# A planner that holds lone attention steps until a second one is ready, and transposes two heads at once

## The chip, the cores and the metric

One Trainium2 chip, one of its cores. The time is the device time of one execution in microseconds (us); a kernel's time is the median of its runs. The kernel before takes 402.29 us (three runs, 402.02 to 402.58). The core has five engines that matter here: TensorE (PE, matrix products and transposes), VectorE (DVE), ScalarE (ACT), GpSimd (POOL) and SyncE (SP, which only issues the DMAs here).

## The reference

The function is a decoder trunk of two layers on 256 tokens of width 1024, in fp32, and a last RMSNorm. Each layer has a mixer and a cross-attention on a memory of 256 rows:

```python
def rms_norm(x, g):
    y = x * lax.rsqrt(jnp.mean(x * x, axis=-1, keepdims=True) + RMS_EPS)
    return y * g
# mixer: one projection of rms_norm(x) to 4096 columns, three attentions beside each other
#   MoBA, 6 heads of 64: at 256 tokens plain causal softmax(q k^T / 8) v
#   differential, 4 heads: (softmax1 - lam * softmax2) v, then a per-head rms_norm
#   stick-breaking, 6 heads: A[t,s] = sigmoid(z_ts) * prod_{s<j<t} (1 - sigmoid(z_tj)), then A v
# each result times silu(its gate columns), all joined; x = x + joined @ w_out
# cross: q = rms_norm(x) @ w_xq, k and v = rms_norm(mem) @ w_xkv, 4 heads of 128, softmax; x = x + ... @ w_xo
```

## The kernel before

**Products.** Each fp32 operand is split in a high and a low part in the reduced type fp32r (`whi`, `wlo` for weights, `xh`, `xl` for activations); each product is made as three, high·high, high·low, low·high. Weights arrive in granules of 128x1024 (`wraw`), each of which ACT turns into `whi` (L155) and DVE into `wlo` (L156). `w_stationary` (L389) makes a group of 512 output columns in 96 products of 256 columns each; `t_stationary` (L416 to L418), `mixed` and the memory projections (L485 to L487 for V) use products of 512 columns.

**What is woven into them.** Attention, norms and score work is written as generators ("jobs"), which the planner in `job`, `tick` and `finish` steps. The planner has a clock `now` in ns of its own. After every 12 products of `w_stationary` the code calls `tick(1310)`, after 6 of `t_stationary` the same, after 3 of the V projection `tick(650)`. A tick adds that to the clock and steps each job whose due time has come, until `JOB_SHARE` ns of work are issued. A step issues its instructions into PE's order at that place, and yields how long it counts for and how long to wait until the next: `PT_WAIT` after the transposes of probabilities, `COMBINE_NEXT` and `MOBA_NEXT` between the first head's and the second head's. `finish(*js)` steps the named jobs to their end with no regard to due times.

The order that comes out is PE's own program order and is fixed before the run. DVE's and ACT's orders are made by a scheduler from its own estimates and from the marks `urgent()`.

**The norm.** A row norm needs the sum of squares over channels. `rstd` does it in two steps. Step A: two transposes of `sqacc` on PE (L350), a reduction on DVE (`ssx`, L353), then `inv_root`: `msx` on DVE (L333), Ln and Exp on ACT (L334, L335), `rtx` in three small operations on DVE (L339 to L341), `rsx` (L342). Step B: two transposes of `rsx` on PE (L358) and a copy to SBUF (`rbcx`, L361), by which projections are multiplied. `rstd` waits `RSTD_WAIT` = 4300 or, in the cross part, `X_RSTD` = 1600 between A and B. In the mixer `finish(njob)` stands behind the gate groups W2 and W3 (192 products, the rest of that norm is forced there), in the cross part behind `memory_v(l, 0)`.

**The mixer.** Order of projections: W2, W3 (gates), W0, M (stick-breaking q, k, v), T0 (differential q, k), T3, T2, T1, the memory's K, then the output O0, O1 in three parts, of which each is preceded by a `finish` of the attention whose results it takes: `finish(*jobs)` for the stick-breaking (`jobs`), `finish(*dj)` for the differential (`dj`), `finish(*mj)` for MoBA (`mj`).

- `sb(c)`: three pairs of heads; scores (`stick_banks`), `softplus` with its splits `sbh`, `sbl` (L168, L169), then `stick_weights` (L620, L621), Exp to `pt`, then values (`pv`, L568 and L570 in all three attentions).
- `diff(c)`: scores (L533), numerators, the combination on DVE, then `p_transposed` for each of two heads (three transposes L557 and the copy to `pt` on ACT, L560), values, the squares' transposes `sums`, and `diff_norm`.
- `moba(c)`: three pairs of heads; scores, numerators, two `p_transposed`, values.

**The cross part.** XQ (96 products), half of V, the forced norm, for each head `xq = bank * rbcx` (L876) and its split, the other half of V woven with score steps (L893 to L902), transposes, `ptl`, then the values (L923), and the output XO or, in the last layer, `last_products` (L988).

In the code and the profile a product number counts projection products of PE from the start, one for each matmul of a projection.

Of the kernel before, what the change touches and what calls it, by code (L numbers as in the profile page):

```python
# [54 lines left out]
ORDER = [(l, g, i) for l in range(DEPTH) for g, i in LAYER]  # L55
N_GRAN = {"O0": 4, "O1": 4, "XQ": 4, "K": 4, "V": 4, "XO0": 2, "XO1": 2}
N_GRAN.update({g: 4 for g in IN_GROUPS})
JOB_SHARE = 1200
SB_WAIT, SB_PACE = 8000, 9000
DIFF_WAIT, DIFF_PACE, COMBINE_WAIT, COMBINE_NEXT = 6500, 8500, 3750, 1700  # L60
MOBA_WAIT, MOBA_PACE, MOBA_NEXT = 5200, 2000, 1100
X_WAIT, PT_WAIT, ROPE_WAIT = 6000, 950, 8800
NORM_WAIT, FIRST_NORM, DN_AFTER = 12500, 10000, 6000
GAINS = dict(attn=0, xattn=16, mem=32)
LOOKAHEAD = 5
# [1 line left out]
Q_WAIT, Q_PACE, XPT_WAIT = 950, 450, 3100  # L67
MEM_WAIT, MEM_NORM, X_RSTD = 6000, 28000, 1600
MOBA_START, SB_START, DIFF_START = 14350, 1500, 1000
PT_LAST = 1300  # L70
MIX_NORM = 14000
HALVED = 5
SQ_WAIT = 5100
# [3 lines left out]
class Trunk:  # L77
# [36 lines left out]
    def tick(self, ns):  # L114

        self.now += ns
        done = 0.0
        for j in list(self.jobs):
            if j[0] <= self.now and done < JOB_SHARE:
                t = self.now  # L120
                self._step(j)
                done += self.now - t
# [505 lines left out]
    def mixer(self, l):  # L628
# [67 lines left out]
        def together(pending, last, first, then):  # L696

            pending.append((first, then))
            if last:
                outs = [f() for f, _ in pending]  # L700
                for o, (_, f) in zip(outs, pending):
                    f(o)
# [34 lines left out]
        def diff(c):  # L737

            self.finish(tj)
            qk = []  # L740
            for s in range(4 * c, 4 * c + 4):
                cb, r = s // 4, 32 * (s % 4)
                qk.append([x[r:r + 32, cb * 256:cb * 256 + 256] for x in dT])
            pr = [self.numerators(ps, 32 ** -0.5) for ps in self.score_quad(qk)]
            yield 1100, DIFF_WAIT
            for j in range(2):
                (p1, r1), (p2, r2) = pr[2 * j:2 * j + 2]
                nc.vector.tensor_scalar(r2, r2, self.lam[:, l:l + 1], None, OP.mult)
                for t, cc in ((0, slice(0, 128)), (1, slice(128, 384))):
                    nc.vector.tensor_scalar(p2[:, cc], p2[:, cc], r2[:, t:t + 1], None, OP.mult)  # L750
                    nc.vector.scalar_tensor_tensor(p1[:, cc], p1[:, cc], r1[:, t:t + 1], p2[:, cc],
                                                   OP.mult, OP.subtract)
            yield 0, COMBINE_WAIT
            pts = []
            for j in range(2):
                pts.append(self.p_transposed(pr[2 * j][0]))
                yield 330, (PT_WAIT if j else COMBINE_NEXT)
            sq = []

            def gated(o):  # L760
                q2 = self.work.tile([128, 256], F32, name="sq")
                nc.scalar.activation(q2, o, AF.Square)
                g = self.gate[3 + len(sq)]
                nc.vector.scalar_tensor_tensor(g, o, self.hg[:, l:l + 1], g, OP.mult, OP.mult)
                sq.append(q2)

            dp.append((pts, c))
            if c == 0:
                return
            outs = [self.pv(lambda j, t: tok["t2"][:, t, 256 + 64 * (2 * c + j):320 + 64 * (2 * c + j)], pts)  # L770
                    for pts, c in dp]
            for o in outs:
                gated(o)
            yield 1440, 2600
            sums = self.bank()
            for i, q2 in enumerate(sq):
                for t in range(2):
                    nc.tensor.transpose(sums[:, i * 256 + t * 128:i * 256 + t * 128 + 128],
                                        q2[:, t * 128:t * 128 + 128], self.ident)
            nc.vector.tensor_reduce(pm, sums.rearrange("p (i d) -> p i d", d=64), AX.X, OP.add)  # L780
            yield 440, 0
# [15 lines left out]
        tok["t3"] = token("T3", "t3")  # L797

        dj = [self.job(diff(c), DIFF_START + DIFF_PACE * c) for c in range(2)]
        t2 = tok["t2"] = token("T2", "t2")  # L800
        self.rope(t2[:, :, 0:256], 4, 64, 8, 0)
# [8 lines left out]
        def moba(c):  # L810
            self.finish(tj2, tj3)
            if c != 1:

                for i in ((0, 1), (), (2,))[c]:
                    qk = [x[64 * j:64 * j + 64] for j in range(2) for x in (blk(i), blk(3 + i))]
                    mq[i] = self.score_banks(*qk)
            ps = []
            for b in mq[c]:
                p, r = self.numerators(b, 0.125)
                for t, cc in ((0, slice(0, 128)), (1, slice(128, 384))):  # L820
                    nc.vector.tensor_scalar(p[:, cc], p[:, cc], r[:, t:t + 1], None, OP.mult)
                ps.append(p)
            yield (1520, 0, 760)[c], MOBA_WAIT
            pts = []
            for j in range(2):
                pts.append(self.p_transposed(ps[j]))
                yield 330, (PT_LAST if j else MOBA_NEXT)
            together(mp, c > 0, lambda: self.pv(lambda j, t: tok["t3"][:, t, 64 * (2 * c + j):64 * (2 * c + j) + 64],
                                                pts),
                     lambda o: nc.vector.tensor_tensor(self.gate[c], o, self.gate[c], OP.mult))  # L830
            yield 640 * len(mp) * (c > 0), 0
            if c:
                mp.clear()

        mj = [self.job(moba(c), MOBA_START + MOBA_PACE * c) for c in range(3)]
        dj.append(self.job(diff_norm(), DN_AFTER))
        self.memory_k(l)
# [274 lines left out]
```

## Time and profile before

| what | value |
|---|---|
| median of 3 runs | 402.29 us (402.02 to 402.58) |
| the profiled execution | 402.34 us, span of its records 400.6 us |
| mean granted clock of TensorE | 0.999 of full speed |
| PE busy | 392.7 us, 98% of the span |
| DVE, ACT busy | 316.1 us (79%), 277.8 us (69%) |
| HBM | 62.55 MB read, 159 GB/s over the span |

The span is 1.74 us shorter than the time of that execution; what lies around it doesn't change with the order of the work. An instruction's start in a timeline is followed by its duration; those of matmuls overlap, so what one costs PE is the distance between two starts. Where a row has `xN`, N instructions of that form follow each other and the duration is of all. In brackets stands how long the engine was idle before the instruction, and who ended that.

### The profile page before, as it was taken

The numbers are of one execution on the slowest core, as the hardware profiler recorded it, in microseconds if no ns is written. First come the engines' busy times: TensorE is split into PE (matmuls) and PEld (weight loads), VectorE is DVE, ScalarE is ACT, GpSimd is POOL, SyncE is SP. The second block draws the span as 40 slices with busy tenths as digits, with TensorE's granted clock in tenths as the row PEclk, the third lists the DMA queues.
The fourth block names the chain that finished last, engine by engine and source line by source line (L and its number), as shares of the span: only waits on it lengthen the run. The fifth ranks groups of instructions, "written<-read, shape, count | busy, mean of one in ns | idle before, by whom it ended". The sixth has DMA issues, their size and how long they took to land.

```text
span 400.6 us, 7730 instructions
## 1 busy us (share of the span) xinstructions
PE 392.7 (98%) x2819; PEld 356.9 (89%) x2819; DVE 316.1 (79%) x786; ACT 277.8 (69%) x587; POOL 41.1 (10%) x105
## 2 busy tenths in 40 slices
PE   8999999999999999999999999999999999999993
PEld 8999988877899989988999999888788999998983
DVE  5978959788967869879796864786997796797964
ACT  7979678776855768549485934879686567674843
POOL 4687930000000000000000000000000000000000
PEclk9999999999999999999999999999999999999999
DMA  8995784433354343721737674443256423361002
GB/s 273 360 321 164 248 318 132 146 107 130 136 179 137 106 148 116 235 82 52 261 116 262 232 234 160 157 159 107 90 160 219 155 91 130 107 205 59 1 2 105
DMA packets 19190, 64.10 MB, mean 160 GB/s; under 512 B 2384, under 2 KB 2768, under 8 KB 19152
## 3 DMA queue, kind: packets, MB, share of 16 engines
q1 hardware_dynamic: 19152, 63.61, 47.2%
q8 instruction: 22, 0.36, 0.4%
q14 instruction: 16, 0.13, 0.1%
HBM read 62.55 MB, written 1.05 MB: 159 GB/s over the span
## 4 chain that ended last, share of the span: by engine, by line
PE 92%; DVE 3%; DMA 2%; ACT 1%; issue 1%; SPq 0%; DVEq 0%; ACTq 0%
PE bank L389 41%; PE bank L416 8%; PE bank L418 7%; PE bank L417 7%; PE bank L988 3%; PE bank L568 2%; PE bank L557 2%; PE bank L923 1%; PE bank L486 1%; PE bank L485 1%; PE bank L487 1%; PE bank L620 1%; DMA wraw<-in_memT_dram 1%; PE bank L726 1%; PE bank L444 1%; PE bank L443 1%
## 5 line engine op out<-in xcount | busy, mean ns | idle before, releaser
L156 DVE TENSOR_TENSOR wlo<-wraw,whi 128x1024 fp32r<-128x1024 f32 (+2 forms) x118 | 137.2, 1169 | 38.7 <-ACT whi L155 38.0
L155 ACT ACTIVATE whi<-wraw 128x1024 fp32r<-128x1024 f32 (+2 forms) x118 | 118.5, 1011 | 41.3 <-PE bank L389 21.0
L389 PE MATMUL bank<-xh,whi 128*128 128x256 f32 x416 | 119.5, 289 | 0.2 <-ACT xh L306 0.2
L389 PE MATMUL bank<-xh,wlo 128*128 128x256 f32 x416 | 117.5, 284 | 0.0
L389 PE MATMUL bank<-xl,whi 128*128 128x256 f32 x416 | 117.1, 283 | 0.0
L389 PEld LDWEIGHTS bank<-xh,whi 128*128 128x128 f32 x416 | 79.8, 193 | 1.7 <-issue 0.7
L389 PEld LDWEIGHTS bank<-xh,wlo 128*128 128x128 f32 x416 | 79.9, 193 | 0.0
L389 PEld LDWEIGHTS bank<-xl,whi 128*128 128x128 f32 x416 | 79.6, 192 | 0.0
L416 PE MATMUL bank<-whi,xh 128*128 128x512 f32 x128 | 52.1, 407 | 0.0
L417 PE MATMUL bank<-wlo,xh 128*128 128x512 f32 x128 | 50.1, 391 | 0.0
L418 PE MATMUL bank<-whi,xl 128*128 128x512 f32 x128 | 50.0, 391 | 0.0
L547 ACT ACTIVATE prob<-prob,mx 128x128 f32<-128x128 f32 (+1 forms) x56 | 24.8, 445 | 10.9 <-DVE mx L544 10.9
L416 PEld LDWEIGHTS bank<-whi,xh 128*128 128x128 f32 x128 | 24.0, 188 | 6.2 <-issue 2.0
L418 PEld LDWEIGHTS bank<-whi,xl 128*128 128x128 f32 x128 | 24.0, 188 | 5.4
L417 PEld LDWEIGHTS bank<-wlo,xh 128*128 128x128 f32 x128 | 24.1, 188 | 4.1
L306 ACT ACTIVATE xh<-h 128x256 fp32r<-128x256 f32 x32 | 14.5, 497 | 6.6 <-DVE h L302 6.3
L389 PE MATMUL bank<-mh,whi 128*128 128x256 f32 x64 | 18.9, 296 | 0.0
L542 DVE CUSTOM_DVE_ANT_0 prob<-bank,cmask 128x128 f32<-128x128 f32 (+1 forms) x56 | 17.9, 351 | 0.3
L389 PE MATMUL bank<-ml,whi 128*128 128x256 f32 x64 | 18.1, 283 | 0.0
L389 PE MATMUL bank<-mh,wlo 128*128 128x256 f32 x64 | 18.1, 282 | 0.0
L317 ACT ACTIVATE sq<-h 128x256 f32<-128x256 f32 x28 | 11.4, 411 | 6.6 <-DVE sqacc L318 6.2
L608 DVE SCALAR_TENSOR_TENSOR sbr<-sbe,sbr 128x384 f32<-128x384 f32 x12 | 6.4, 555 | 11.8 <-ACT sbr L607 11.8
(268 smaller groups left out, 780.0 us busy)
## 6 DMA issues: line engine op xcount, KB each, us to landing
wraw<-in_w_dram SPq DMA_DIRECT2D x107, 512.0 KB, 3.6
wraw<-in_w_dram SPq DMA_DIRECT2D x10, 256.0 KB, 4.6
wraw<-in_memT_dram SPq DMA_DIRECT2D x4, 512.0 KB, 4.8
h<-in_xT_dram SPq DMA_DIRECT2D x3, 256.0 KB, 4.9
out_dram<-wraw SPq DMA_DIRECT2D x2, 288.0 KB, 2.2
wraw<-in_gfin_dram SPq DMA_DIRECT2D x1, 512.0 KB, 4.7
out_dram<-wraw SPq DMA_DIRECT2D x2, 224.0 KB, 2.2
h<-in_xT_dram SPq DMA_DIRECT2D x1, 280.0 KB, 3.2
```

The costliest lines, as they stand in the source:

```text
L155: nc.scalar.activation(hi[:, c], raw[:, c], AF.Copy)
L156: nc.vector.tensor_tensor(lo[:, c], raw[:, c], hi[:, c].bitcast(F32), OP.subtract)
L306: nc.scalar.activation(h, src[k], AF.Copy, scale=g)
L317: nc.scalar.activation(s, src[k], AF.Square)
L389: nc.tensor.matmul(outs[m], st[:, kk, c], x[k], start=k + p == 0 and m % 2 == 0, stop=k == n - 1 and p == 2, skip_group_check=True)
L416: nc.tensor.matmul(outs[t], xh[k][:, c], whi[:, kk, :], start=first, stop=False)
L417: nc.tensor.matmul(outs[t], xh[k][:, c], wlo[:, kk, :], start=False, stop=False)
L418: nc.tensor.matmul(outs[t], xl[k][:, c], whi[:, kk, :], start=False, stop=last)
L542: nc.vector.tensor_tensor_reduce(s[:, c], ps[:, c], self.cmask[:, c], 1.0, -3.0e38, OP.add, OP.max, accum_out=m[:, t:t + 1])
L547: nc.scalar.activation(s[:, c], s[:, c], AF.Exp, bias=m[:, t:t + 1], scale=scale, accum_out=sm[:, t:t + 1])
L557: nc.tensor.transpose(ps[:, b * 128:b * 128 + 128], p[:, b * 128:b * 128 + 128], self.ident)
L988: nc.tensor.matmul(out[:, 0:w], x[:, r], w_, start=m == 0 and not seeded, stop=m == 11, skip_group_check=True)
```

## The change

`tick` looks first at how many jobs are due. If it is exactly one, and it came due less than `HOLD` = 2700 ns ago by the planner's clock, the tick does nothing. Otherwise it steps as before. `finish` is not touched. In `diff` and `moba` the transposes of both heads are issued in one step, at the time at which the second head's was issued before or, by the hold, later. `PT_WAIT` goes from 950 to 1400, `PT_LAST` from 1300 to 1500.

```diff
-JOB_SHARE = 1200
+JOB_SHARE, HOLD = 1200, 2700
...
-X_WAIT, PT_WAIT, ROPE_WAIT = 6000, 950, 8800
+X_WAIT, PT_WAIT, ROPE_WAIT = 6000, 1400, 8800
...
-PT_LAST = 1300
+PT_LAST = 1500
...
         self.now += ns
+        ready = [j[0] for j in self.jobs if j[0] <= self.now]
+        if len(ready) == 1 and self.now - ready[0] < HOLD:
+            return
         done = 0.0
...
             yield 0, COMBINE_WAIT
-            pts = []
-            for j in range(2):
-                pts.append(self.p_transposed(pr[2 * j][0]))
-                yield 330, (PT_WAIT if j else COMBINE_NEXT)
+            yield 0, COMBINE_NEXT
+            pts = [self.p_transposed(pr[2 * j][0]) for j in range(2)]
+            yield 660, PT_WAIT
...
             yield (1520, 0, 760)[c], MOBA_WAIT
-            pts = []
-            for j in range(2):
-                pts.append(self.p_transposed(ps[j]))
-                yield 330, (PT_LAST if j else MOBA_NEXT)
+            yield 0, MOBA_NEXT
+            pts = [self.p_transposed(p) for p in ps]
+            yield 660, PT_LAST
```

Every engine has the same instructions as before; only their order differs. On PE the stretches of other work between projection products become 52, from 67. The line numbers of the kernel after are 3 higher (L350 is L353 there, L358 is L361, L389 is L392).

First place: the norm of the mixer in layer 0, where group W3 ends and W0 begins. PE before (`xh_303`, `xl_304` are the last channel block of W3, `xh_275` the first of W0); step A stands 48 products earlier:

```order
L389 MATMUL bank<-xh_303,whi 128x256
L389 MATMUL bank<-xh_303,wlo 128x256
L389 MATMUL bank<-xl_304,whi 128x256
L358 MATMUL bank<-ident,rsx 128x128 x2
L389 MATMUL bank<-xh_275,whi 128x256
L389 MATMUL bank<-xh_275,wlo 128x256
L389 MATMUL bank<-xl_276,whi 128x256
```

PE after, the same place:

```order
L392 MATMUL bank<-xh_303,whi 128x256
L392 MATMUL bank<-xh_303,wlo 128x256
L392 MATMUL bank<-xl_304,whi 128x256
L353 MATMUL bank<-ident,sqacc 128x128 x2
L361 MATMUL bank<-ident,rsx 128x128 x2
L392 MATMUL bank<-xh_275,whi 128x256
L392 MATMUL bank<-xh_275,wlo 128x256
```

Step A has moved to the forced `finish`, directly in front of step B. DVE before, from the reduction of step A on:

```order
L353 TENSOR_REDUCE ssx<-bank 128x2
L156 TENSOR_TENSOR wlo<-wraw,whi 128x1024
L333 TENSOR_SCALAR msx<-ssx 128x2
L156 TENSOR_TENSOR wlo<-wraw,whi 128x1024
L339 TENSOR_TENSOR rtx<-rsx 128x2
L340 TENSOR_TENSOR rtx<-rtx,msx 128x2
L341 TENSOR_SCALAR rtx<-rtx 128x2
L156 TENSOR_TENSOR wlo<-wraw,whi 128x1024
L342 TENSOR_TENSOR rsx<-rsx,rtx 128x2
L156 TENSOR_TENSOR wlo<-wraw,whi 128x1024
L361 COPY rbcx<-bank 128x256
```

DVE after (`ml` is the low part of the memory's activations, which before stood behind `rbcx`); `ssx` and one `wlo` stand ahead of these rows:

```order
L336 TENSOR_SCALAR msx<-ssx 128x2
L310 SCALAR_TENSOR_TENSOR ml_634<-wraw,h,mh_633 128x256
L310 SCALAR_TENSOR_TENSOR ml_638<-wraw,h,mh_637 128x256
L310 SCALAR_TENSOR_TENSOR ml_642<-wraw,h,mh_641 128x256
L342 TENSOR_TENSOR rtx<-rsx 128x2
L310 SCALAR_TENSOR_TENSOR ml_646<-wraw,h,mh_645 128x256
L343 TENSOR_TENSOR rtx<-rtx,msx 128x2
L310 SCALAR_TENSOR_TENSOR ml_650<-wraw,h,mh_649 128x256
L344 TENSOR_SCALAR rtx<-rtx 128x2
L310 SCALAR_TENSOR_TENSOR ml_654<-wraw,h,mh_653 128x256
L345 TENSOR_TENSOR rsx<-rsx,rtx 128x2
L310 SCALAR_TENSOR_TENSOR ml_658<-wraw,h,mh_657 128x256
```

Six operations of the memory's split now stand between `msx` and `rsx`. Second place: ACT in layer 0 while the third pair of stick-breaking heads is made ready (`sbh` is its split, `t_1303` the token group T3). Before:

```order
L607 ACTIVATE sbr<-sby 128x384
L728 ACTIVATE dT_1149<-bank 128x512
L155 ACTIVATE whi<-wraw 128x1024
L168 ACTIVATE sbh<-sbe 128x384
L686 ACTIVATE t_1303<-bank,rsx 128x512 x2
L168 ACTIVATE sbh<-sbe 128x384
L728 ACTIVATE dT_1150<-bank 128x512
L155 ACTIVATE whi<-wraw 128x1024
L624 ACTIVATE pt<-bank 128x384 x2
```

And after:

```order
L731 ACTIVATE dT_1102<-bank 128x512
L608 ACTIVATE sby<-sbe 128x384
L689 ACTIVATE t_1303<-bank,rsx 128x512
L171 ACTIVATE sbh<-sbe 128x384
L610 ACTIVATE sbr<-sby 128x384
L689 ACTIVATE t_1303<-bank,rsx 128x512
L158 ACTIVATE whi<-wraw 128x1024
L627 ACTIVATE pt<-bank 128x384
L171 ACTIVATE sbh<-sbe 128x384
L627 ACTIVATE pt<-bank 128x384
```

The second head's `sbr` and `sbh` have moved behind the two halves of `t_1303` and a `whi`. Third place: PE in the cross part of layer 0, in the first half of the V projection. Before:

```order
L487 MATMUL bank<-whi,ml_646 128x512
L350 MATMUL bank<-ident,sqacc 128x128 x2
L485 MATMUL bank<-whi,mh_649 128x512
L486 MATMUL bank<-wlo,mh_649 128x512
L487 MATMUL bank<-whi,ml_650 128x512
L485 MATMUL bank<-whi,mh_653 128x512
L486 MATMUL bank<-wlo,mh_653 128x512
L487 MATMUL bank<-whi,ml_654 128x512
L485 MATMUL bank<-whi,mh_657 128x512
L486 MATMUL bank<-wlo,mh_657 128x512
L487 MATMUL bank<-whi,ml_658 128x512
```

And after:

```order
L490 MATMUL bank<-whi,ml_658 128x512
L488 MATMUL bank<-whi,mh_661 128x512
L489 MATMUL bank<-wlo,mh_661 128x512
L490 MATMUL bank<-whi,ml_662 128x512
L353 MATMUL bank<-ident,sqacc 128x128 x2
L361 MATMUL bank<-ident,rsx 128x128 x2
L488 MATMUL bank<-whi,mh_633 128x512
L489 MATMUL bank<-wlo,mh_633 128x512
```

Step A has moved 12 products later, to the end of the first half of V, and step B follows it at once; before, nine products stood between them (step B follows the last row of the first of these two). In layer 1 the cross part moves alike.

## Rows read from the trace of the kernel before

**Rows 1.** Page: busy time by engine; share of the chain that ended last

```profile
PE 392.7 (98%) x2819; PEld 356.9 (89%) x2819; DVE 316.1 (79%) x786; ACT 277.8 (69%) x587; POOL 41.1 (10%) x105
...
PE 92%; DVE 3%; DMA 2%; ACT 1%; issue 1%; SPq 0%; DVEq 0%; ACTq 0%
```

**Rows 2.** Windows behind the last product: window, us, busy by engine, PEclk, DMA, GB/s

```profile
394.50:399.50 5.00, 0.00 (x0) 0.00 (x0) 1.53 (x6) 1.65 (x5) 0.00 (x0) 1.00 0.34 130
399.50:400.60 1.10, 0.00 (x0) 0.00 (x0) 0.00 (x0) 0.00 (x0) 0.00 (x0) 0.50 0.00 0
```

**Rows 3.** Chain in order of time, 136 to 150: start us, us, what

```profile
138.24 0.66 PE bank L557 x6
...
143.84 1.63 PE bank L389 x12
145.47 0.33 PE bank L557 x3
145.80 1.43 PE bank L389 x12
```

**Rows 4.** Timeline of PE, first norm: start us, us, instruction

```profile
23.23 0.38 PE L350 MATMUL bank<-ident,sqacc 128*128 128x128 f32 x2
23.37 0.36 PE L389 MATMUL bank<-xh,whi 128*128 128x256 f32 x1
...
29.20 0.38 PE L358 MATMUL bank<-ident,rsx 128*128 128x128 f32 x2
```

**Rows 5.** Timeline of DVE, first norm

```profile
23.65 0.42 DVE L353 TENSOR_REDUCE ssx<-bank 128x2 f32<-128x256 f32 x1 [1.68 <-PE bank L350]
24.00 1.26 DVE L156 TENSOR_TENSOR wlo<-wraw,whi 128x1024 fp32r<-128x1024 f32 x1
25.18 0.16 DVE L333 TENSOR_SCALAR msx<-ssx 128x2 f32<-128x2 f32 x1
...
30.42 3.24 DVE L307 SCALAR_TENSOR_TENSOR ml<-wraw,h,mh 128x256 fp32r<-128x256 f32 x8
```

**Rows 6.** Timeline of ACT, first norm

```profile
29.32 3.31 ACT L306 ACTIVATE mh<-wraw,h 128x256 fp32r<-128x256 f32 x8
```

**Rows 7.** Timeline of PE, norm of the cross part, layer 0

```profile
170.96 0.38 PE L350 MATMUL bank<-ident,sqacc 128*128 128x128 f32 x2
...
173.33 0.43 PE L358 MATMUL bank<-ident,rsx 128*128 128x128 f32 x2
```

**Rows 8.** Timeline of DVE, cross part, layer 0

```profile
173.11 0.16 DVE L342 TENSOR_TENSOR rsx<-rsx,rtx 128x2 f32<-128x2 f32 x1
...
175.00 0.48 DVE L494 SCALAR_TENSOR_TENSOR xvl<-bank,rsm,xv 128x256 fp32r<-128x256 f32 x1
...
181.58 1.21 DVE L156 TENSOR_TENSOR wlo<-wraw,whi 128x1024 fp32r<-128x1024 f32 x1
```

**Rows 9.** Timeline of PE, third stick-breaking pair, layer 0

```profile
84.88 0.34 PE L620 MATMUL bank<-sbh,trim 128*128 128x384 f32 x1
```

**Rows 10.** Timeline of DVE, third stick-breaking pair, layer 0

```profile
81.60 1.21 DVE L156 TENSOR_TENSOR wlo<-wraw,whi 128x1024 fp32r<-128x1024 f32 x1
...
84.39 0.56 DVE L169 TENSOR_TENSOR sbl<-sbe,sbh 128x384 fp32r<-128x384 f32 x1
```

**Rows 11.** Timeline of ACT, third stick-breaking pair, layer 0

```profile
82.56 1.38 ACT L686 ACTIVATE t<-bank,rsx 128x512 f32<-128x512 f32 x2 [0.79 <-PE bank L418]
```

**Rows 12.** Page, costliest groups: count | busy us, mean ns | idle before, releaser

```profile
L155 ACT ACTIVATE whi<-wraw 128x1024 fp32r<-128x1024 f32 (+2 forms) x118 | 118.5, 1011 | 41.3 <-PE bank L389 21.0
```

**Rows 13.** Instructions of line 560: duration min/median/max in ns, first and last start

```profile
L560 ACT ACTIVATE pt<-bank x20: 469/477/491, 103.1 to 340.2; 128x384 f32<-128x384 f32 x20
```

**Rows 14.** Chain, its longest pieces, cross parts of layers 0 and 1

```profile
174.25 0.76 DVE xq L876 x2
...
383.44 11.07 PE bank L988 x60
```

**Rows 15.** Timeline of ACT, norm of the mixer, layer 1

```profile
218.81 0.91 ACT L306 ACTIVATE mh<-wraw,h 128x256 fp32r<-128x256 f32 x2 [1.19 <-DMA wraw<-in_memT_dram]
```

## The prediction

> **What bounds the kernel now.** I read the page's busy times first, then its chain, then timelines of PE, DVE and ACT at each place where PE's order changes. PE is busy for 392.7 of 400.6 us and has 92% of the chain that ended last [rows 1]: nearly everything waits for PE, and PE waits for hardly anything. So the change can gain only by making PE's own work shorter, and it loses wherever a held step makes PE wait, because the products behind a waiting instruction can't pass it. At most 400.6 − 392.7 = 7.9 us of idle PE can go, of which some 6 us are the tail after the last product [rows 2], which the change doesn't touch.
>
> The chain also gives the price of a stop. Six transposes cost 0.66 us and three 0.33, 0.11 each with no fixed part [rows 3]: joining two stops of three saves nothing on PE. Twelve products take 1.43 us, and 1.63 where they follow a values step in fp32 [rows 3]: such a stop has 0.20 us that joining could save.
>
> **The change part by part.** The order of the kernel after gives the places; the prices are from the rows.
>
> A, norm of the mixer, layer 0. Before, step A is at 23.23 and step B at 29.20 [rows 4], with 48 products between, which cost 29.20 − 23.37 = 5.8 us (the two transposes cost PE 23.37 − 23.23 = 0.14 by the next start; their row's 0.38 overlaps). PE never waits there. After, B follows A at once, and PE stands for the whole chain. From A's start: the reduction begins 0.42 later (23.65 − 23.23) [rows 4, 5], takes 0.35 until the next begins; `wlo` takes 1.18 (25.18 − 24.00) [rows 5]; `msx` is thus at +1.95. Behind it DVE's new order has three `ml`, 3.24 / 8 = 0.405 each [rows 5], which end at about +3.3; ACT's Ln and Exp lie beside them, behind `mh` of 3.31 / 8 = 0.41 [rows 6]. Then `rtx`, `ml`, `rtx`, `ml`, `rtx`, `ml`, `rsx`: three `ml` and some 0.15 for each small one bring `rsx` to +4.95. From `rsx` to B it is 0.22 (173.33 − 173.11) [rows 7, 8]: B starts at +5.17. Of this A's own 0.14 was paid before: **+5.0** on PE, with nothing that hides it. If the `ml` come late and the scheduler's order leaves only `wlo` in the way, it is 4.0; with three `mh` ahead of Ln and one `wlo` of waiting, 5.6.
>
> B, third pair of stick-breaking heads, layer 0 (the T3 group's end). Before, the second head's `sbl` began at 84.39 and took 0.56; PE began the block at 84.88 [rows 9, 10], just as it became ready: no slack. After, the block is behind the end of T3 and six products; its weights need the second head's `sbr` and `sbh`, which ACT now has behind the two halves of `t` (1.38) [rows 11], a `whi` of 1.01 [rows 12], and DVE behind a `wlo` of 1.21 [rows 10]. Counted from T3's last product, PE comes to the second head's part at 3.5 and its high part is ready at 5.65, its low part at 6.15: I take **+2.5**. The lower end is 0 (DVE's chain `sbr`, `sbe` isn't delayed if ACT reorders nothing that matters), the upper 3.5, with one more `wlo`. In layer 1 the same pair comes 12 products later and is covered: 0.
>
> C, the differential heads. Both heads' transposes now come together, and values, squares and `diff_norm` 36 products later, in front of the second part of the output, with 48 products left (5.7 us by 1.43 for 12 [rows 3]). The norm of 8 columns, two multiplications and two splits fit under that: 0. If that cover were gone, 0 to 1 in each layer.
>
> D, the last MoBA pair, both layers. Before, twelve products stood between the last head's transposes and its values [rows 3]. After, the forced `finish` puts six transposes directly in front of the values; PE waits for both `pt` copies on ACT, 0.477 us each [rows 13], one behind the other, of which the first begins while PE transposes the second head: 0.33 to fill and 0.477 to leave, **+0.8** each, **1.6** together. With a `whi` ahead of them on ACT it would be 3; with the copies early, 0.6. Queued behind are the last parts of O0 and O1, which need these values.
>
> E, norm of the cross part, both layers. Before, nine products covered most of A to B (170.96 to 173.33) [rows 7], and what followed was a chain on DVE, not on PE: `xq` is a piece of the chain that ended last [rows 14]. After, A comes 12 products later and B at once behind it. A chain bound by latency moves by what its head moves: 12 products of V (nine of them take 2.2 between these rows, some 0.1 of it a restart behind the transposes; twelve take 12 / 9 × 2.1 = 2.8 us), and what PE stands between A and B (173.33 − 170.96 − 0.14 = 2.2) lies inside this. Added to it: an `xvl` of 0.48 and, on its path, part of a `wlo` of 1.21 [rows 8], which the new order has ahead of the splits of `xq` and of `ptl`: 0.6 and 0.6. **+4.0** in layer 0; in layer 1, where last_products follow (11.07) [rows 14] and one `wlo` less is in the way, **+3.6**. Together 7.6; from 5 (only the 2.2 each, and 0.3 of order) to 9.
>
> F, norm of the mixer, layer 1. Here `mh` waited for a DMA of the memory until 218.81 [rows 15], and B waited for it. After, A is 24 products later and B 12 later, so 36 instead of 48 stand between: 4.5 us by program; seven `ml`, two `wlo` (1.2 each) and a `whi` put `rsx` at about +6.1: a stall of 1.6, of which 0.3 was there before: **+1.3**, from 0 (the DMA had set it all) to 2.5.
>
> G, the joined stops. Of fifteen stops less, two have the exit of 0.20 [rows 3]: **−0.4**, from 0 to −1.
>
> Sum: 5.0 + 2.5 + 0 + 1.6 + 4.0 + 3.6 + 1.3 − 0.4 = **+17.6**. On the profiled execution of 402.34 this is **419.9**; the median of the runs, 402.29, is 0.05 below, which doesn't matter here. With all lower ends 4.0 + 0 + 0 + 0.6 + 5 + 0 − 1 = +8.6, **411**; with all upper ends 5.6 + 3.5 + 2 + 3 + 9 + 2.5 + 0 = +25.6, **428**.
>
> **The rivals.**
> The clock falls. PE's granted clock went from 1.00 to 0.50, its lower level of 1.2 GHz, after 5.0 us without a product [rows 2]; the whole run before has no other such fall. In A the gap is 5.17 − 0.38 = 4.8 us, nearly as long. If the lower level holds for as long as the gap, some 5 us, about 21 products run where 42 would, and 2.5 us are lost: **422.4**. For it: the likeness of the gaps; against it: no gap under 5.0 us that fell is in the rows, and E's are only 2.2.
> The Trainium skill, "TensorE: Matmul & The Clock Gate", section "Why this matters for your kernels", says that idle gaps between bursts of products put the array back to the lower clock. The trace agrees for the gap at its end; by that rule A costs 422.4, without it 419.9.
>
> Only the norms cost. The queues of DVE and ACT have some slack (79% and 69% busy [rows 1]) and a PE that waits 5 us lets them catch up, so B and D are covered, and the cross part gives only its stall of 2.2 in each layer: 5.0 + 2.2 + 2.2 + 0.5 = 9.9, **412.3**. Against it: B has no slack in the rows [rows 9, 10], and D's copies can't begin before PE's transposes.
>
> Fewer stops win. If each stop had an entry and exit of 0.35 (0.20 from [rows 3] and an entry of 0.15 that I estimate from the same step), fifteen fewer would save 5.2 and, with every wait covered, give **397.1**, faster than before. It decides as soon as the waits sum to less than the saving. Against it: what is joined are transposes, whose six cost twice what three do [rows 3], and A's wait alone is as much.
>
> Nothing moves: the waits are absorbed and nothing is saved, 402.3. That would need products between A and B that the order doesn't have.
>
> **How the numbers follow.** Forecast 0.61, the clock 0.19, only the norms 0.13, fewer stops 0.03, nothing 0.04. What this measurement can tell from no change is about 0.2%, 0.8 us. The first three are all slower by over 0.2%: 0.93, and with the half of "nothing" that falls on that side 0.94. Faster has the 0.03 of fewer stops, and the rest, 0.03, is within. The time given is that of the forecast. The range is from 411 to 428: the bounds of the sum, which hold the clock's and the norms' cases; outside stay the last two cases and a tenth of the first, about 2 in 10.
>
> **What the profile after would show.** A: PE idle for some 5 us between lines 353 and 361 near 29 us, ended by DVE's `rsx`; the granted clock in the next window tells whether it fell. E: about 2.2 us idle in front of line 361 near 180 and 375, then the scores and `ptl` in the chain by 2 to 4 us later than PE's products alone would put them. B: PE idle in front of the stick weights (line 623) near 90. D: PE idle of about 0.8 behind line 560's six transposes, ended by ACT's `pt`. F: idle in front of line 361 in layer 1. PE's busy sum should stay within 1 us of 392.7. Wrong I would be if PE waited nowhere in A, which needs another order of DVE on the chip than the program has, or if the busy sum of PE fell by 5 us.

## The result, and the profile after

The kernel after takes 426.87 us (five runs, 425.83 to 428.44) against 402.06 (401.85 to 402.58, five runs beside it) for the kernel before: a ratio of 1.0615, 95% interval 1.0599 to 1.0631, 24.8 us slower. The range of 411 to 428 holds it; 419.9, the sum of the waits, is 7 us short. The runs also lie further apart than before's: 2.6 us from lowest to highest, against 0.7.

The page of the profiled execution after (426.24 us, span 424.5), with the lines that answer to [rows 1]:

```profile
PE 398.9 (94%) x2819; PEld 360.7 (85%) x2819; DVE 317.0 (75%) x786; ACT 278.4 (66%) x587; POOL 38.8 (9%) x105
...
PE 76%; ACT 10%; DVE 10%; issue 3%; DMA 1%; ACTq 0%; DVEq 0%
```

Only PE is busy for much longer, by 6.2 us, and not with more work (x2819 in both): some of it runs at half the clock, below. The chain that ended last passed from PE (92% before) to ACT and DVE, which had 4% together and now have 20%: PE waits for them. The view of waits on PE says where (who waited, for what: us in total, times, the longest):

```profile
PE bank L361 <- DVE rsx L345: 10.9, 4, 4.5
PE bank L623 <- ACT sbh L171: 2.5, 1, 2.5
PE bank L560 <- DVE mx L545: 2.5, 2, 1.2
PE bank L889 <- DVE xql L172: 1.6, 2, 0.8
PE bank L1040 <- DVE warm L1017: 1.2, 1, 1.2
PE bank L571 <- ACT pt L563: 0.6, 2, 0.3
```

The wait of the warm-up (L1040) stands before as well; all others are new or, for the norms, were 0.2 us in all. The first row is the norms (terms A, E, F), the second the stick-breaking pair (B), the third and the last MoBA (D), the fourth the cross scores (E).

The first norm on PE, which answers to [rows 4]:

```profile
29.03 0.38 PE L353 MATMUL bank<-ident,sqacc 128*128 128x128 f32 x2
...
33.88 0.43 PE L361 MATMUL bank<-ident,rsx 128*128 128x128 f32 x2 [4.46 <-DVE rsx L345]
```

B starts 4.85 us after A. DVE's queue between them, which answers to [rows 5]:

```profile
29.45 0.42 DVE L356 TENSOR_REDUCE ssx<-bank 128x2 f32<-128x256 f32 x1 [2.70 <-PE bank L353]
29.79 1.22 DVE L159 TENSOR_TENSOR wlo<-wraw,whi 128x1024 fp32r<-128x1024 f32 x1
30.92 0.17 DVE L336 TENSOR_SCALAR msx<-ssx 128x2 f32<-128x2 f32 x1
31.00 1.26 DVE L310 SCALAR_TENSOR_TENSOR ml<-wraw,h,mh 128x256 fp32r<-128x256 f32 x3
...
33.64 0.18 DVE L345 TENSOR_TENSOR rsx<-rsx,rtx 128x2 f32<-128x2 f32 x1
```

`rsx` is at A + 4.61 where 4.95 was forecast. And then the clock fell. Windows of the same execution (columns as in [rows 2]: the last but two is the granted clock): the gap, what follows it, what follows that; then the same for the gap at the stick-breaking pair:

```profile
29.50:33.50 4.00, 0.00 (x0) 0.00 (x0) 4.00 (x12) 2.36 (x8) 3.33 (x9) 1.00 0.72 262
34.50:38.25 3.75, 3.75 (x21) 3.75 (x20) 3.54 (x11) 3.74 (x11) 2.92 (x11) 0.54 0.02 4
38.50:42.00 3.50, 3.50 (x32) 3.50 (x31) 3.08 (x12) 3.47 (x7) 3.01 (x9) 1.00 0.37 124
91.75:94.00 2.25, 0.03 (x1) 0.00 (x0) 1.81 (x3) 0.87 (x3) 0.00 (x0) 1.00 0.01 4
96.00:99.50 3.50, 3.50 (x16) 2.59 (x9) 3.00 (x23) 2.22 (x11) 0.00 (x0) 0.51 0.02 5
```

In 3.75 us at a mean of 0.54 PE made 21 products, in the 3.50 us at full clock behind it 32. Here the clock fell only after PE was at work again, not in the gap. (1 − granted clock) times the window is 1.7 us for each of the two falls; that is an upper bound for what a fall costs. By the starts of the same products against before's, each of these two cost 1.5 (the lag grows from 4.7 to 6.2 behind the first, from 3.1 to 4.6 behind the second, counted from ahead of that block). The gap at 91.75 was only 2.50 us long. Between A and B of the cross norms PE waited about as long, 2.6 us, and in this execution the clock stood at 1.00 behind both (189.75 and 390.50). So the gap's length alone does not say whether the clock falls.

### The profile page after: what moved, and what is told of

The parts are those of the page before. It is cut to its first block, busy times and chain, and to the rows that moved or that the text cites. A ratio compares the mean times of both kernels' runs of the same rounds, so it can differ in the third digit from the quotient of the medians.

```text
span 424.5 us, 7737 instructions
## 1 busy us (share of the span) xinstructions
PE 398.9 (94%) x2819; PEld 360.7 (85%) x2819; DVE 317.0 (75%) x786; ACT 278.4 (66%) x587; POOL 38.8 (9%) x105
## 4 chain that ended last, share of the span: by engine, by line
PE 76%; ACT 10%; DVE 10%; issue 3%; DMA 1%; ACTq 0%; DVEq 0%
PE bank L392 33%; PE bank L419 7%; PE bank L420 6%; PE bank L421 6%; ACT whi L158 4%; DVE wlo L159 3%; PE bank L989 3%; PE bank L571 2%; ACT prob L550 2%; PE bank L490 1%; PE bank L488 1%; PE bank L489 1%; PE bank L924 1%; DMA wraw<-in_memT_dram 1%; PE bank L560 1%
## 5 line engine op out<-in xcount | busy, mean ns | idle before, releaser
L392 PE MATMUL bank<-xh,whi 128*128 128x256 f32 x416 | 119.9, 290 | 0.0
L392 PE MATMUL bank<-xh,wlo 128*128 128x256 f32 x416 | 118.3, 286 | 0.0
L392 PE MATMUL bank<-xl,whi 128*128 128x256 f32 x416 | 118.1, 285 | 0.0
L392 PEld LDWEIGHTS bank<-xh,whi 128*128 128x128 f32 x416 | 80.6, 195 | 1.5 <-issue 0.7
L392 PEld LDWEIGHTS bank<-xh,wlo 128*128 128x128 f32 x416 | 80.7, 195 | 0.0
L392 PEld LDWEIGHTS bank<-xl,whi 128*128 128x128 f32 x416 | 80.7, 195 | 0.0
L550 ACT ACTIVATE prob<-prob,mx 128x128 f32<-128x128 f32 (+1 forms) x56 | 24.8, 443 | 12.9 <-DVE mx L547 12.7
L392 PE MATMUL bank<-mh,whi 128*128 128x256 f32 x64 | 18.8, 294 | 0.0
L392 PE MATMUL bank<-ml,whi 128*128 128x256 f32 x64 | 18.1, 283 | 0.0
L392 PE MATMUL bank<-mh,wlo 128*128 128x256 f32 x64 | 18.1, 283 | 0.0
L321 DVE TENSOR_TENSOR sqacc<-sqacc,sq 128x256 f32<-128x256 f32 x35 | 14.8, 424 | 0.9 <-ACT sq L320 0.2
```

The costliest lines, as they stand in the source:

```text
L321: nc.vector.tensor_tensor(sq, sq, s, OP.add)
L392: nc.tensor.matmul(outs[m], st[:, kk, c], x[k], start=k + p == 0 and m % 2 == 0, stop=k == n - 1 and p == 2, skip_group_check=True)
L550: nc.scalar.activation(s[:, c], s[:, c], AF.Exp, bias=m[:, t:t + 1], scale=scale, accum_out=sm[:, t:t + 1])
```

## The experiments

Three kinds: what was held is let go, one job at a time; the gaps are filled with products that nobody reads, to leave the waits and take the clock's fall away; the change is cut in two. Medians are of four runs (five and eleven for the two with more rounds), beside 402.1 to 402.4 for before on the same chip.

**One job let go at a time.** In `tick`, with another name for each:

```diff
-        ready = [j[0] for j in self.jobs if j[0] <= self.now]
-        if len(ready) == 1 and self.now - ready[0] < HOLD:
+        ready = [j for j in self.jobs if j[0] <= self.now]
+        if len(ready) == 1 and self.now - ready[0][0] < HOLD and ready[0][1].__name__ not in ("norm",):
             return
```

> After's kernel, but the mixer's norm job is never held, so its steps A and B stand 48 products apart again in both layers; everything else on PE stays where the change put it. Theory 1 (each wait costs by itself, and nothing else takes it up): the 4.9 us stall of layer 0 goes, with it the clock's fall behind it (1.5 us) and the 1.5 us of layer 1: 426.9 - 7.9 = 419.0, and the clock stays at 1.00 from 29 to 96 us. Rival (the queues of DVE and ACT take a later wait up: while PE stood they caught up): half of it comes back elsewhere, 423.

Measured 419.31 (418.02 to 420.59), ratio 1.0417 [1.0397, 1.0437]: 7.6 us less than after, as theory 1 had it. The first product behind A comes 4.7 us earlier. But the clock did not stay up: in the profiled run it fell for 7.0 us at the stick-breaking pair and once more behind the cross norm of layer 1, by the windows up to 5.1 us lost in sum, against 3.4 in after's profile. The sum came out right with a share of luck.

```profile
84.00:88.25 4.25, 1.75 (x10) 1.36 (x9) 3.55 (x7) 2.68 (x5) 0.00 (x0) 1.00 0.10 13
88.50:95.50 7.00, 6.91 (x31) 4.98 (x30) 4.31 (x29) 3.91 (x16) 0.00 (x0) 0.51 0.18 68
```

The first of these windows of that kernel holds the gap, the second the fall.

The cross part's job is told by identity (`ready[0] is not self.free`, where `cross` sets `self.free = njob`).

> After's kernel, but the norm job of the cross part is never held: step A 9 products ahead of step B again, in both layers; nothing else moves on PE. Theory 1 (the whole chain of the cross part moves with its head): 3.6 us in layer 0 and 3.9 in layer 1 go, 426.9 - 7.5 = 419.4. Rival (only PE's stall between A and B costs, the rest is the order of the scores): 2 x 2.8 = 5.6, 421.3. Rival 2 (waits are taken up elsewhere): 424.

Measured 420.28 (418.88 to 420.95), ratio 1.0447 [1.0423, 1.0471]: 6.6 less, between theory 1 (7.5) and the rival (5.6). Here too the clock's falls come to 5.1 us in the profiled run (by the windows), and layer 0 kept a wait of 1.2 in front of the transposes of its probabilities. Left to the steady clock below.

With `"sb"` for the name:

> After's kernel, but the stick-breaking jobs are never held; their steps stand at before's places again in both layers, the memory's norm step B 6 products earlier, all else as after. Theory 1: the stall of 3.1 us at the third pair of layer 0 goes, and with it the second fall of the clock (1.3 us behind it); layer 1 gives back the 0.5 it had gained: 426.9 - 3.9 = 423.0, clock 1.00 from 40 us on. Rival (the clock falls there for the low activity of these fp32 products and not for the stall): 3.1 - 0.5 = 2.6 go, 424.3.

Measured 424.02 (421.56 to 425.33), ratio 1.0537 [1.0498, 1.0577]. The median lies between the two. At the place itself theory 1 holds: the wait is gone and the clock stays at 1.00 behind the pair. But it fell for 7.0 us at A and behind both cross norms, so the sum can't be read:

```profile
33.00:40.00 7.00, 6.15 (x29) 6.15 (x30) 6.65 (x19) 6.95 (x16) 5.74 (x17) 0.51 0.22 78
186.50:190.25 3.75, 3.75 (x12) 2.95 (x11) 2.23 (x6) 1.71 (x3) 0.00 (x0) 0.54 0.00 0
388.00:391.50 3.50, 3.50 (x11) 2.73 (x10) 2.03 (x5) 1.17 (x2) 0.00 (x0) 0.51 0.00 0
```

With `"moba"`:

> After's kernel, but the MoBA jobs are never held: six transposes at 744, 756 and 768 instead of twelve at 756 and six directly in front of the last values; nothing else moves on PE. Theory 1 (the fourth group of transposes waits for a PSUM bank that DVE has not yet read, 1.2 us, and the values wait for pt, 0.8, with what hangs on both 2.6 in each layer): 426.9 - 5.1 = 421.8. Rival (the prediction's term D: only the wait for pt, 0.8 in each layer): 425.3.

Measured 426.26 (425.55 to 428.19), ratio 1.0608 [1.0581, 1.0635]: no gain that the runs can tell. Theory 1 fell. The wait for the PSUM bank (L560, `mx`, in after's list) is gone, but one as long has taken its place, at the joined transposes of the third pair:

```profile
PE bank L560 <- DVE prob L823: 2.5, 2, 1.3
```

The transposes of two heads in one step wait for the later head's probabilities, or for a bank that a later pair's maximum (`mx`) has not yet read: both are DVE being late for the last of what the step joins. The wait for `pt` (L571, 0.6 in after) has gone from the list. By the starts of the same products, MoBA now costs 1.6 in each layer where it costs 2.3 in after, so 0.7 in each layer is given back, near the rival's 0.8. That the medians show only 0.6 of these 1.3 is put down to the clock: in this profiled run (428.19) it fell four times, up to 8.5 us by the windows, against 3.4 in after's.

**The gaps filled.** In `rstd`, between A and B, and likewise 24 of 128 columns between the two heads' `stick_weights`:

```diff
+        for i in range((24 if name == 'x' and wait != X_RSTD else 12) if fill is not None else 0):
+            nc.tensor.matmul(ps[:, 256:512], fill[:, 0:128], fill, start=True, stop=True, skip_group_check=True)
         yield 220, wait
```

> After's kernel with products whose results nobody reads put into the gaps in which PE waits: 24 of 256 columns between steps A and B of the mixer's norm in layer 0, 24 of 128 columns between the two heads' weights of layer 0's third stick-breaking pair, 12 of 256 columns between A and B of both cross norms. Theory 1 (the clock falls because PE stands, and the fall costs beside the wait): the waits end when they did, the clock stays at 1.00 up to the last product, some 4 us go, about 423, and the runs lie within 1 us of each other. Rival (it falls for what PE does before and after, sparse fp32 work, or the fall costs nothing as the waits end later anyway): 426.9, runs as far apart as after's.

Measured 423.35 (423.17 to 423.76), ratio 1.0522 [1.0508, 1.0536]. Theory 1 holds in all parts but one: the runs lie within 0.6 us, the clock is at 1.00 up to the last product, and 72 more products made the kernel 3.5 us faster than after. The windows that answer to the two falls:

```profile
34.50:38.25 3.75, 3.75 (x33) 3.75 (x33) 3.63 (x13) 3.74 (x11) 2.92 (x12) 1.00 0.06 21
92.00:100.00 8.00, 8.00 (x62) 6.38 (x61) 5.21 (x31) 4.87 (x19) 0.00 (x0) 1.00 0.20 66
```

33 products in the 3.75 us in which after made 21. The step B of the first norm comes where it came (A + 4.90, 4.85 in after).

The part that fails is the wait at the stick-breaking pair, which the filling itself made longer. ACT's `sbh` was done at 92.68, but the 24 products stood in front of PE's next block:

```profile
92.16 0.52 ACT L172 ACTIVATE sbh<-sbe 128x384 fp32r<-128x384 f32 x1 [1.38 <-DVE sbe L616]
```

```profile
90.82 2.90 PE L719 MATMUL bank<-xh 128*128 128x128 f32 x24 [0.60 <-ACT pt L630]
93.56 0.39 PE L626 MATMUL bank<-sbh,trim 128*128 128x384 f32 x1
```

The lag against before grows there by 3.5, where it grows by 3.0 to 3.1 in four executions with this gap unfilled, read at the first product behind the block, before a fall could add to it (after, cross_free, moba_free, hold_only). So some 0.4 of this kernel's time is the filling's own, and the clock's share of after is rather 3.9 than 3.5.

This kernel has a steady clock, so its trace gives the bare price of each wait, but for the 0.4 at B. The start of the same projection product against before's, read ahead of and behind each place:

| term | forecast | layer 0 | layer 1 | sum |
|---|---|---|---|---|
| A, mixer norm, layer 0 | 5.0 | 5.0 | | 5.0 |
| B, third stick-breaking pair | 2.5 | 3.4 | 0 | 3.4 |
| D, MoBA | 1.6 | 2.3 | 2.3 | 4.6 |
| E, cross part | 7.6 | 4.1 | 3.9 | 8.0 |
| F, mixer norm, layer 1 | 1.3 | | 0.9 | 0.9 |
| C, G and the rest | −0.4 | −0.4 | −0.3 | −0.7 |
| all | 17.6 | | | 21.2 |

Of the −0.4 in the last but one row 0.3 is no gain: this trace is that much ahead of before's already in front of A.

On top of this kernel two jobs were let go again:

> The kernel with filled gaps (clock at 1.00 throughout, 423.35), and the mixer's norm not held, its filling taken out. Theory 1 (with a steady clock the price is the bare wait): 4.9 in layer 0 and 1.5 in layer 1 go, 423.35 - 6.4 = 416.9. Rival (later waits take a part up): 418 to 420.

Measured 417.73 (417.45 to 417.96), ratio 1.0387 [1.0371, 1.0402]: 5.6 less. Behind A the offset to before is 0.05 where it was 4.67. At F the offset falls by 0.4 where it grew by 0.9, so F gives 1.3, against the 1.5 that after's trace had suggested. Nothing later takes it up: 4.6 + 1.3 = 5.9 is the difference of the two profiled executions (423.51 and 417.63); the medians lie 5.6 apart. The rival fell.

> The kernel with filled gaps (423.35), and the cross part's norm not held, its filling taken out. Theory 1 (what the cross part loses is the wait between A and B and the wait of its scores for the splits, 3.9 us in each layer as the offsets of after's trace have it): 423.35 - 7.8 = 415.5. Rival (the 3.2 us between A and B alone, less the stop before): 423.35 - 5.7 = 417.7.

Measured 416.87 (416.79 to 420.58; the other three end at 416.90), ratio 1.0388 [1.0345, 1.0432]: 6.5 less, between the two. The run of 420.58 has a mean granted clock of 0.987 where the others have 0.998 and 0.999: in that run the clock fell in spite of the filling; it isn't the profiled one, so where it fell is open. Layer 1 gives back all of its 3.9. Layer 0 gives 2.9 and keeps 1.2, as a wait that the order of before did not have:

```profile
PE bank L917 <- DVE prob L912: 1.2, 1, 1.2
```

Its scores stand at 993 and 996 as in after's order, so only 12 V products lie between them and these transposes, where before had 15. So in layer 0 1.2 of E goes with the order of the scores, in layer 1 nothing. In after itself the scores wait 0.8 in each layer for `xql`, which has a `wlo` ahead of it on DVE, as the prediction's E had it; with the norm let go that wait is gone in both layers.

```profile
192.57 1.23 DVE L159 TENSOR_TENSOR wlo<-wraw,whi 128x1024 fp32r<-128x1024 f32 x1 [0.22 <-ACT whi L158]
193.72 0.76 DVE L172 TENSOR_TENSOR xql<-xq,xqh 128x256 fp32r<-128x256 f32 x2
```

> The kernel with filled gaps (423.35), and the memory's split of layer 0 issued behind the projection W0 instead of behind the forced norm, so that no ml stands in DVE's queue between the norm's steps; in their place DVE has one wlo more. Theory 1 (the wait of A is DVE's queue: three ml of 0.4 behind msx, three more between the small operations, against one wlo of 1.2): B comes 3.8 us after A instead of 4.8, 422.3, if the later memory norm costs nothing. Rival (the wait is ACT's Ln and Exp and semaphores, not the queue): still 4.8, 423.35.

In the diff, `self.memory_split(l)` moves behind `outs = self.w_stationary(l, "W0", xs)` where `l` is 0. Measured 423.85 (423.41 to 424.28), ratio 1.0543 [1.0525, 1.0561]. At the place itself theory 1 holds: DVE has one `wlo` and no `ml` between `msx` and the three `rtx`, and B comes 3.98 us after A.

```profile
30.80 0.20 DVE L337 TENSOR_SCALAR msx<-ssx 128x2 f32<-128x2 f32 x1
30.92 1.21 DVE L160 TENSOR_TENSOR wlo<-wraw,whi 128x1024 fp32r<-128x1024 f32 x1
32.05 0.15 DVE L343 TENSOR_TENSOR rtx<-rsx 128x2 f32<-128x2 f32 x1
...
32.67 0.16 DVE L346 TENSOR_TENSOR rsx<-rsx,rtx 128x2 f32<-128x2 f32 x1
```

Of the 0.9 gained there half is lost again in the trace before the third pair, where the steps of the memory's norm now stand 30 and 24 products later, and the medians show no gain. The queue is shown to set 0.9 of the wait's 4.9; that this is worth something in the end is not shown, and the other 4.0 are not taken apart by any run.

**The change cut in two.** `HOLD = 0`:

> The change without its hold (HOLD = 0): both heads' transposes in one step and the two waits, nothing else; norms, stick-breaking and scores stand where they stood before. Theory 1 (the joined step waits for the later head): the third MoBA pair's transposes wait 1.3 us for its second head's probabilities as they did where MoBA alone was free, 1.6 us net in each layer: 402.1 + 3.2 = 405.3, clock 1.00 throughout. Rival (that wait came from DVE being late behind the held steps): 402.1.

Measured 404.80 (404.10 to 405.35), ratio 1.0059 [1.0046, 1.0072]: 2.4 slower than before's 402.39. Theory 1 holds, with 0.9 for each wait and not 1.3; the offset to before grows by 1.3 at MoBA in each layer, and nowhere else. PE's waits, all of them:

```profile
PE bank L560 <- DVE prob L823: 1.8, 2, 0.9
PE bank L1040 <- DVE warm L1017: 1.2, 1, 1.2
```

Of it, the differential heads alone (`diff` as in the change, with the old `PT_WAIT`):

> Before's kernel, of the change only the differential heads' transposes joined: two stops of six instead of four of three in each layer, nothing else moves. Theory 1 (six transposes cost twice what three do, nothing waits): 402.1, no change. Rival (each stop has a fixed part of 0.3 us): four fewer save 1.2, 400.9.

Measured 402.01 (eleven runs, 401.36 to 403.00), ratio 0.9986 [0.9974, 0.9997], less than 0.2% from no change: theory 1. Four stops fewer save no 1.2 us (0.4 by the medians, 0.1 in the trace). So what no_hold loses is MoBA's.

And the other half:

> Before's kernel with the hold alone; transposes and waits as before. Theory 1 (the hold makes the waits of the norms and of the stick-breaking pair, the joined step makes MoBA's): 4.9 + 3.1 + 7.5 + 1.5 and some 3 to 4 for the clock, less 0.5: 402.1 + 20 = 422. Rival (MoBA's waits are the hold's too): 426 or more.

Measured 426.67 (424.76 to 428.06), ratio 1.0600 [1.0572, 1.0628]. Neither theory is right as it stands, though the rival's number is met. MoBA loses 0.7 in layer 0 and 2.6 in layer 1, where the hold by itself brings nine transposes together twice and one group waits 1.4 for `prob`; so layer 1's wait is the hold's as well. These 3.3 are most of the 4.7 above 422; the rest is put down to the clock, which in the profiled run (428.06) fell at every one of the four gaps (A, B and both cross norms), up to 8.5 us by the windows, where theory 1 had 3 to 4.

## Why the prediction was right where it was, and where not

The direction, the range and the mechanism were right: the chain passed from PE to the engines it waits for, at the places named (A, B, D, E, F), and the joined stops saved next to nothing. That 426.87 still lies within the range is in part luck: the waits alone came to 423.35 at a steady clock (0.4 of it the filling's), the clock's 3.5 or more was in no term of the sum, and the upper end of 428 was added up from upper ends of other terms, of which D went beyond its own and the others stayed below theirs. The sign given for PE's busy sum, within 1 us of 392.7, failed: it is 398.9. And the cases that the forecast leaves outside its range add up to 0.13, not to 2 in 10. By its steps:

- A: forecast +5.0, measured 5.0 (4.67 and the 0.29 by which that trace starts earlier). fill_split_late shows a part of it, 4.90 to 3.98, to be the `ml` in DVE's queue; the rest is read from the trace, and no run tested it.
- B: 2.5 taken; 3.0 to 3.1 in the unfilled executions, 3.4 in the table with the filling's 0.4, both within the bound of 3.5. PE stood for 2.50 of it. The forecast's 3.5, 5.65 and 6.15 stand without their working. What the chain after shows: `sbe` of the second head (L613) ran only behind that `wlo`, and `sbh` behind `sbe`.

```profile
91.00 0.96 ACT whi L158
...
91.98 1.22 DVE wlo L159
93.20 0.48 DVE sbe L613
...
93.71 0.53 ACT sbh L171
```

- C and G: no wait of PE in after is at the differential heads, so C's 0 holds. G is not shown by itself: without the 0.3 of the start, all that the table's row holds is −0.4, and diff_joined saved 0.1 in its trace.
- D is the term that was mis-sized: 1.6, measured 4.6, with 3 as its upper end. The step that failed is "PE waits for both `pt` copies on ACT": that wait is there, but 0.3 each, where 0.8 was forecast. What it left out is the wait of the transposes themselves, for a PSUM bank or for the later head's probabilities, 1.2 in each layer. These two are 1.5 of the 2.3 in each layer; the other 0.8 no run separates. The prediction priced the end of the joined step, not its inputs: two operands in one step make it wait for the later. It looked only at where the values moved and took the transposes, which moved later, as safe.

```profile
149.91 1.15 PE L560 MATMUL bank<-ident,prob 128*128 128x128 f32 x9
152.28 0.55 PE L560 MATMUL bank<-ident,prob 128*128 128x128 f32 x3 [1.23 <-DVE mx L545]
```

In layer 0 after, nine transposes run and the last three wait. That they waited for a bank, which the row infers from who had read it, is supported by moba_free only in so far as that wait went when the place changed.

- E: 8.0 for 7.6, and F 0.9 for 1.3.
- The clock was a rival, put at 422.4 with 0.19, and it came true besides the forecast: 426.87 − 423.35 = 3.5 us, in the median, 3.9 without the filling's 0.4. What failed is treating it as a case of its own with one gap. Gaps as short as 2.2 were set aside, as no row showed them to matter. With a gap of 2.5 at the stick-breaking pair the clock fell there in all five profiled executions that have it unfilled.

The Trainium skill, "TensorE: Matmul & The Clock Gate", section "Why this matters for your kernels", says that idle gaps beyond a certain length between bursts of products return the array to its lower clock. The traces agree for A's gap of 4.5 us in five executions out of five. The Trainium skill's limit lies above the gaps of 2.5 us at the stick-breaking pair and of 2.6 at the cross norms, and these were followed by a fall too, in five out of five and in seven out of ten: here the traces decide.

The case "only the norms cost" is excluded by B and D, "fewer stops win" by diff_joined, "nothing moves" by the result itself.

## What to carry to other kernels

Where one engine has the chain and its order is fixed, moving a step to where it has company is free only if what it waits for is ready there, and what waits for it is still far off; a hold must end early enough that a forced finish doesn't meet both halves of a two-step chain. A step that joins two operands is as late as the later one: price its inputs as well as its results. And where waits bring gaps into a dense stream of products, ask for the granted clock in the windows behind them: a wait can be paid a second time there, and by a different amount in each run.

## What the runs showed that was not expected

Products that nobody reads made the kernel faster, by 3.5 us (426.87 to 423.35), and brought the runs from 2.6 to 0.6 us of each other: the spread of after was the clock's. A fall filled a window of 3.5 to 3.75 us or one of 7.0 us, and its begin is not tied to the gap's end: in four executions that begin lay within A's gap (at 32.1 to 33.1, of a gap from 29.4 to 33.9 or within 0.4 of that), in after behind it, and at the stick-breaking pair of after some 1.7 us after PE had gone back to work (94.28, clock down from 96.00 on). The same gap of 2.6 us at the cross norms was followed by a fall in some executions and not in others: none of two in after, one of two in norm_free, both in sb_free, moba_free and hold_only. What decides between them stays open.
